# Turning the residual stream into channel order with VectorE's 32 by 32 transposes instead of TensorE's

## The chip, the core and the metric

The kernel runs on one core of one Trainium2 chip. The core's engines work beside each other, each through its own queue in order: TensorE (PE, matmuls; its weight loads are shown as PEld), VectorE (DVE), ScalarE (ACT), GpSimd (POOL) and SyncE (SP, which issues most transfers). They wait for each other through semaphores. The metric is the device time of one execution in microseconds (us), the median over several runs. An engine's memory has 128 partitions; a group of 32 of them is called a quadrant here.

## The reference

Two layers over 256 tokens of width 2048 in float32. Layer 0 mixes tokens with a convolution module, layer 1 with latent attention; after each comes an MLP with a squared ReLU.

```python
for layer in range(DEPTH):                       # DEPTH = 2
    h = rms_norm(x, norm_mixer_g[layer])
    if layer % 2 == 0:
        x = x + conv_module(h, ...)              # ends in u @ w_pw2 + b_pw2
    else:
        x = x + mla(h, ...)                      # ends in o @ w_o
    h = rms_norm(x, norm_mlp_g[layer])
    x = x + jnp.square(jax.nn.relu(h @ w1)) @ w2
return rms_norm(x, final_norm_g)
```

## The kernel before

The residual `x` stays on the chip for the whole run as `xs`, in token order: 128 partitions, two tiles of 128 tokens (t = 0, 1), 2048 channels. A matmul that consumes it needs it in channel order, with channels on the partitions: the buffers `xt`, four of them, one for each block of 512 channels (n = 0 to 3). A block holds four groups k of 128 channels, each with 256 tokens.

Products are computed to float32 accuracy out of parts of lower precision. Each operand x is split into an upper part `hi` = round(x) (ACT, line 161 for weights, line 200 for activations) and a lower part `lo` = x - hi (DVE, line 165 for weights, line 207 for activations that are scaled by a gain). Three matmuls then add up: hi times hi, hi times lo, lo times hi (`mm3`, lines 194 to 196, and lines 409 and 410 in the MLP's first product, where hi and lo lie side by side).

Weights come from memory in units of four groups k of 512 columns (1 MB), by SP into `raw` (three buffers). Each unit is split in two halves, and there are six buffers of halves for `hi` and for `lo` (`WB = 6`). One half is read by 12 matmuls in the products that write tokens on the partitions, and by 16 in the MLP's first product.

Three stages end in a sum onto the residual and turn it into channel order for the next: the convolution module's last product (`conv_w_pw2`), the MLP of layer 0 (the second half of `mlp_w2`) and the attention's output (`mla_w_o`). They share `residual_stage` and `product_A`:

- `product_A` goes over blocks n. For each it computes two accumulators (t = 0, 1) over all k, then DVE adds them to `xs` (`add`, lines 331 and 333).
- `prepare(n)` turns block n into channel order. It is not called at once: the block is put on the list `due`, and `prepare` is called for all blocks on it after the first weight unit of the next block, so that the work stands behind matmuls that don't need it. The last block is turned after the product.
- In the convolution module and in the attention the blocks 0 and 1 are computed before, in one go, and `product_A` is called for blocks 2 and 3 with `due = (0, 1)`: both are turned inside block 2.
- `to_T` (line 252 and following) turns two groups k: four transposes of 128x128 by PE into a bank of PSUM (`tr`), then two upper parts by ACT (line 200) and two lower parts by DVE (line 207), each times the gain of the next norm. A block is two calls: eight transposes, four upper parts, four lower parts.
- `prepare` then also squares the block on ACT (line 345) for the next norm's sum.

In these stages the order of the instructions on each engine's queue is set by a scheduler at build time. The mixers' inner parts are ordered by hand.

At the start of layer 1 some small memsets on DVE (lines 1094 to 1098) and copies on ACT fill the rows for the attention mask; the first product there (`mla_w_in`) takes weights with 576 columns, whose halves hold one group k each.

Of the kernel before, what the change touches and what calls it, by code (L numbers as in the profile page):

```python
# [10 lines left out]
F32 = mybir.dt.float32  # L11
# [7 lines left out]
P = 128  # L19
D = 2048  # L20
KC = D // P
T = 2
S = T * P
FF = 4 * D
NB = 512
# [10 lines left out]
HALVES = 2  # L36
# [41 lines left out]
def trunk_kernel(  # L78
# [26 lines left out]
    nc = tc.nc  # L105
# [27 lines left out]
    def nm(s):  # L133
        uid[0] += 1
        return f"{s}_{uid[0]}"


    def acc_tile():
        return psum["acc"].tile([P, NB], F32, tag="acc", name=nm("acc"))

    def tr_tile():
        return psum["tr"].tile([P, NB], F32, tag="tr", name=nm("tr"))
# [40 lines left out]
    def load_split(srcs, nj):  # L183
        return split(load(srcs, nj), nc.vector)

    def rows(w, k0, nk, c0, n):

        return w[k0 * P : (k0 + nk) * P, c0 : c0 + n].rearrange(
            "(j p) n -> p j n", p=P
        )  # L190
# [7 lines left out]
    def hi_part(ps, hi, scale=1.0):  # L198

        nc.scalar.activation(hi, ps, AF.Copy, scale=scale)  # L200

    def lo_part(ps, hi, lo, scale=None):

        if scale is None:
            nc.vector.tensor_tensor(lo, ps, hi.bitcast(F32), op=ALU.subtract)
        else:
            nc.vector.scalar_tensor_tensor(
                out=lo, in0=ps, scalar=scale, in1=hi.bitcast(F32), op0=ALU.mult, op1=ALU.subtract
            )
# [37 lines left out]
    def to_T(src, k0, hi, lo, gain):  # L247

        pt = tr_tile()
        for j in range(2):  # L250
            for t in range(T):
                nc.tensor.transpose(  # L252
                    pt[:, j * S + t * P : j * S + (t + 1) * P],
                    src[:, t, (k0 + j) * P : (k0 + j + 1) * P],
                    ident,
                )
        ps = [pt[:, j * S : (j + 1) * S] for j in range(2)]
        for j in range(2):
            hi_part(ps[j], hi(k0 + j), gain[:, k0 + j : k0 + j + 1])
        for j in range(2):  # L260
            lo_part(ps[j], hi(k0 + j), lo(k0 + j), gain[:, k0 + j : k0 + j + 1])
# [4 lines left out]
    xs = main.tile([P, T, D], F32, name="xs")  # L266
# [26 lines left out]
    g_mix, g_mlp, b_pw1, b_dw, ln_g, ln_b, g_q, g_kv = cols  # L293
    g_mix = [g_mix[:, 0:KC], g_mix[:, KC:]]
    g_mlp = [g_mlp[:, 0:KC], g_mlp[:, KC:]]


    xt_cx, xt = [ExitStack()], []

    def right_pool(name, bufs):  # L300

        xt_cx[0].close()
        xt_cx[0] = ExitStack()
        return xt_cx[0].enter_context(tc.tile_pool(name=name, bufs=bufs, side="right", reuse_waits="tile"))
# [3 lines left out]
    def open_xt(name):  # L308
        pool = right_pool(name, 1)
        xt[:] = [  # L310
            pool.tile([P, KC // NNB, 2 * S], F32R, name=nm("xt")) for _ in range(NNB)
        ]

    xhl = lambda k: xt[k // 4][:, k % 4, :]
    xh = lambda k: xhl(k)[:, :S]
    xl = lambda k: xhl(k)[:, S:]
# [3 lines left out]
    xh_kt = lambda k, t: xh(k)[:, t * P : (t + 1) * P]  # L320
    xl_kt = lambda k, t: xl(k)[:, t * P : (t + 1) * P]

    def residual_stage(last, gain, r_scale=None):


        ssq = small.tile([P, T, NNB], F32, tag="ssq", name=nm("ssq")) if last else None

        def add(n, ps, t):
            sl = slice(n * NB, (n + 1) * NB)
            if r_scale is None:  # L330
                nc.vector.tensor_tensor(xs[:, t, sl], ps[t], xs[:, t, sl], op=ALU.add)
            else:
                nc.vector.scalar_tensor_tensor(
                    out=xs[:, t, sl], in0=ps[t], scalar=r_scale[:, t : t + 1], in1=xs[:, t, sl],
                    op0=ALU.mult, op1=ALU.add,
                )

        def prepare(n, only=None):
            sl = slice(n * NB, (n + 1) * NB)
            if last:  # L340
                if gain is not None:
                    for j in range(2):
                        to_T(xs, 4 * n + 2 * j, xh, xl, gain)
                for t in range(T) if only is None else [only]:
                    nc.scalar.activation(scratch, xs[:, t, sl], AF.Square, accum_out=ssq[:, t, n : n + 1])

        return ssq, add, prepare
# [41 lines left out]
    def mlp(layer, ssq, next_gain, finish=None, before=None):  # L389

        with ExitStack() as cx:
            mp = cx.enter_context(tc.tile_pool(name=f"mp{layer}", bufs=1, reuse_waits="tile"))
            nkh = FF // P // HALVES
            r2 = small.tile([P, T], F32, tag="r2", name=nm("r2"))
            nssq = None
            for hf in range(HALVES):
                hh, hl = [], []
                for g in range(nkh // 4):
                    ps = [acc_tile() for _ in range(4)]
                    c0 = (hf * nkh + 4 * g) * P  # L400
                    for u in range(KC // 4):
                        wj = load_split([rows(mlp_w1[layer], 4 * u, 4, c0, NB)], 4)
                        for j in range(4):
                            k = 4 * u + j
                            wh, wl = wj(j)
                            for b in range(4):
                                bs = slice(b * P, (b + 1) * P)

                                nc.tensor.matmul(ps[b], wh[:, bs], xhl(k), start=k == 0, stop=False)  # L409
                                nc.tensor.matmul(ps[b][:, :S], wl[:, bs], xh(k), start=False, stop=k == KC - 1)  # L410
                    gh = mp.tile([P, 4, S], F32R, tag="gh", name=nm("gh"), bufs=nkh // 4)
                    gl = mp.tile([P, 4, S], F32R, tag="gl", name=nm("gl"), bufs=nkh // 4)
                    for b2 in range(2):
                        v = mp.tile([P, 2, S], F32, tag="v", name=nm("v"), bufs=2)
                        for b in range(2):
                            o = ps[2 * b2 + b]
                            nc.scalar.activation(v[:, b, :], o[:, S:], AF.Copy)  # L417
                            nc.vector.tensor_tensor(v[:, b, :], o[:, :S], v[:, b, :], op=ALU.add)
                        nc.vector.scalar_tensor_tensor(out=v, in0=v, scalar=0.0, in1=v, op0=ALU.max, op1=ALU.mult)
                        bs = slice(2 * b2, 2 * b2 + 2)  # L420
                        nc.scalar.activation(gh[:, bs, :], v, AF.Copy)
                        nc.vector.tensor_tensor(gl[:, bs, :], v, gh[:, bs, :].bitcast(F32), op=ALU.subtract)
                    hh.append(gh)
                    hl.append(gl)
                if hf == 0:
                    r = rms_rstd(ssq, NNB, D, "n")
                    nc.vector.tensor_tensor(r2, r, r, op=ALU.mult)
                nssq, add, prepare = residual_stage(hf == HALVES - 1, next_gain, r2)
                product_A(
                    mlp_w2[layer],  # L430
                    hf * nkh,
                    nkh,
                    lambda k, t: hh[k // 4][:, k % 4, t * P : (t + 1) * P],
                    lambda k, t: hl[k // 4][:, k % 4, t * P : (t + 1) * P],
                    add,
                    prepare,
                    finish=(lambda t: finish(nssq, t)) if finish is not None and hf == HALVES - 1 else None,
                    before=lambda: before(nssq),
                )
            return nssq  # L440


    with ExitStack() as cx:
# [16 lines left out]
        ca = cv.tile([P, KC, S], F32, tag="tok", name="ca")  # L460
# [208 lines left out]
        with tc.manual_schedule():  # L669
# [36 lines left out]
            for t in range(T):  # L706
# [6 lines left out]
                out=ms0[:, 0:1], in0=xmv[:, 0:1], scalar=xmv[:, 0:1], in1=xmv[:, 1:2], op0=ALU.mult, op1=ALU.add  # L713
# [39 lines left out]
            first, last = ((0, 0), (0, 1)), ((1, 0),)  # L753
# [47 lines left out]
            for c in range(1, KC + 1):  # L801
                n = UC * c
# [88 lines left out]
            for m in range(NP):  # L891
# [4 lines left out]
                for j in range(2):  # L896
                    k = 2 * m + j
# [17 lines left out]
                for q in {NP - 3: (0, 1, 4), NP - 2: (5, 2, 3), NP - 1: (6, 7)}.get(m, ()):  # L915
                    t, i = divmod(q, NNB)
                    sl = slice(i * NB, (i + 1) * NB)
                    nc.vector.tensor_tensor(xs[:, t, sl], xs[:, t, sl], b2[:, sl], op=ALU.add)

        ssq, add, prepare = residual_stage(True, g_mlp[0])  # L920
        for b in range(2):
            for t in range(T):
                add(b, ps2[b], t)
# [3 lines left out]
    with tc.tile_pool(name="rt", bufs=1, reuse_waits="tile") as rt:  # L927
# [52 lines left out]
        nc.scalar.activation(cos, an2, AF.Sin)  # L980

    ssq = mlp(0, ssq, g_mix[1])


    with ExitStack() as cx:
# [321 lines left out]
        with tc.manual_schedule():  # L1307
# [9 lines left out]
            for k in range(KC):  # L1317
                u, j = divmod(k, 2)
# [15 lines left out]
            for k in range(KC):  # L1334
                u, j = divmod(k, 4)
# [30 lines left out]
            cq = at.tile([P, T, QR], F32, tag="cx", name="cq")  # L1366
# [28 lines left out]
            for g in range(NG):  # L1395
                for i in range(HG):
                    h = g * HG + i

                    n = -(-len(work) // (HG - i))
# [29 lines left out]
            prefetch()  # L1429

        open_xt("xt1")
        ssq, add, prepare = residual_stage(True, g_mlp[1])
        for b in range(2):
            for t in range(T):
                add(b, ps_o[b], t)
# [3 lines left out]
    with tc.tile_pool(name="fin", bufs=1, reuse_waits="tile") as fp:  # L1439
# [35 lines left out]
        def before(ssq):  # L1475

            for t in range(T):
# [4 lines left out]
                for n in range(NNB - 1):  # L1482
                    gained(t, n)

        mlp(1, ssq, None, finish, before)


# [24 lines left out]
```

## Time and profile before

| | |
|---|---|
| median of 3 runs | 1991.07 us (1990.93 to 1991.36) |
| profiled execution, its own time | 1991.4 us |
| its span, first to last instruction | 1989.6 us |
| granted TensorE clock, mean | 0.998 |
| instructions | 27809 |

The profile is of one execution. Busy time of an engine is time in which it had an instruction at work; matmuls overlap each other, so a row's "mean ns of one" is longer than the distance between two. In a group of rows the columns are line, engine, operation, output and inputs with shapes, count, then busy time in us and mean ns of one, then the idle time of the engine in front of them and what ended it. In a timeline the columns are start, length (of the merged instructions), engine, line, operation, and in brackets the idle time before and what ended it. The view of waits shows who waited for whom: total us, times, longest.

### The profile page before, as it was taken

What the parts mean: (1) busy time and instruction counts of PE and PEld (TensorE: products, weight loads), DVE (VectorE), ACT (ScalarE), POOL (GpSimd) and SP (SyncE); (2) the same over time, 40 slices, a digit from 0 to 9 for tenths busy, and PEclk for the clock granted to TensorE, in tenths of its full rate; (3) what the DMA queues carried; (4) which work ended last, traced back from release to release, by engine and by line L of the source; (5) the groups of instructions that cost most, each with busy time, mean ns of one, the idle gap of its engine ahead of it and who ended that gap; (6) DMA issues with size and microseconds to landing.
All of it is one profiled execution on the core that took longest, in us unless ns stands there. A gap on an engine that the chain in (4) does not pass through costs nothing.

```text
span 1989.6 us, 27809 instructions
## 1 busy us (share of the span) xinstructions
PE 1969.4 (99%) x11042; PEld 1728.2 (87%) x11042; DVE 1219.7 (61%) x1796; ACT 973.5 (49%) x1377; POOL 228.0 (11%) x189
## 2 busy tenths in 40 slices
PE   8999999999999999999999999999999999999998
PEld 8999888888888888888899998888888888888886
DVE  6999976566444556655556666556654445665553
ACT  5456755454333444544456655545443334454442
POOL 6999300000000000000001310000000000000000
PEclk9999999999999999999999999999999999999999
DMA  7666465565556666665555445666656566665553
GB/s 240 186 181 185 148 205 180 190 190 190 194 195 196 191 189 189 191 198 182 190 167 161 129 141 187 196 189 190 189 195 197 197 192 189 189 190 194 191 190 106
DMA packets 243585, 367.57 MB, mean 185 GB/s; under 512 B 15480, under 2 KB 89984, under 8 KB 243200
## 3 DMA queue, kind: packets, MB, share of 16 engines
q1 hardware_dynamic: 242416, 363.67, 57.7%
q10 hardware_dynamic: 1040, 2.13, 0.3%
q8 instruction: 86, 1.41, 0.3%
q14 instruction: 43, 0.35, 0.0%
HBM read 363.68 MB, written 2.10 MB: 184 GB/s over the span
## 4 chain that ended last, share of the span: by engine, by line
PE 91%; DVE 6%; ACT 1%; POOL 1%; issue 0%; DMA 0%; ACTq 0%; POOLq 0%; DVEq 0%
PE acc L409 23%; PE acc L194 15%; PE acc L196 15%; PE acc L195 15%; PE acc L410 12%; DVE sum L580 5%; PE acc L500 2%; PE acc L908 2%; PE tr L252 1%; POOL lo L165 1%; PE sum L550 0%; ACT hi L161 0%; PE acc L1286 0%; DMA xs<-in_x 0%; PE acc L1150 0%
## 5 line engine op out<-in xcount | busy, mean ns | idle before, releaser
L165 DVE TENSOR_TENSOR lo<-raw,hi 128x1024 fp32r<-128x1024 f32 (+2 forms) x630 | 760.7, 1211 | 691.0 <-ACT hi L161 679.3
L161 ACT ACTIVATE hi<-raw 128x1024 fp32r<-128x1024 f32 (+1 forms) x696 | 722.9, 1046 | 788.0 <-PE acc L195 446.1
L409 PE MATMUL acc<-xt,hi 128*128 128x512 f32 x2048 | 710.6, 390 | 0.0
L410 PE MATMUL acc<-xt,lo 128*128 128x256 f32 x2048 | 577.7, 282 | 0.0
L409 PEld LDWEIGHTS acc<-xt,hi 128*128 128x128 f32 x2048 | 384.4, 188 | 80.5
L194 PE MATMUL acc<-hi,gh 128*128 128x512 f32 x1024 | 398.6, 389 | 0.0
L196 PE MATMUL acc<-lo,gh 128*128 128x512 f32 x1024 | 398.4, 389 | 0.0
L195 PE MATMUL acc<-hi,gl 128*128 128x512 f32 x1024 | 398.4, 389 | 0.0
L410 PEld LDWEIGHTS acc<-xt,lo 128*128 128x128 f32 x2048 | 387.1, 189 | 0.1
L196 PEld LDWEIGHTS acc<-lo,gh 128*128 128x128 f32 x1024 | 192.2, 188 | 40.3
L194 PEld LDWEIGHTS acc<-hi,gh 128*128 128x128 f32 x1024 | 192.2, 188 | 39.7
L195 PEld LDWEIGHTS acc<-hi,gl 128*128 128x128 f32 x1024 | 192.2, 188 | 39.5
L500 PE MATMUL acc<-xt,hi 128*128 128x256 f32 x1024 | 178.9, 281 | 0.0
L580 DVE SCALAR_TENSOR_TENSOR sum<-ub,w_dw,sum 128x256 f32<-128x256 f32 x395 | 160.4, 484 | 3.9 <-ACT sum L556 2.9
L165 POOL TENSOR_TENSOR lo<-raw,hi 128x1024 fp32r<-128x1024 f32 x66 | 157.4, 2406 | 23.5 <-ACT hi L161 19.5
L500 PEld LDWEIGHTS acc<-xt,hi 128*128 128x128 f32 x1024 | 154.4, 188 | 0.1
L500 PE MATMUL acc<-xt,lo 128*128 128x256 f32 x512 | 138.7, 280 | 0.3 <-POOL lo L165 0.3
L500 PEld LDWEIGHTS acc<-xt,lo 128*128 128x128 f32 x512 | 94.3, 188 | 0.5 <-POOL lo L165 0.5
L1081 POOL MEMSET pad_kv<- 128x8 f32 x1 | 0.1, 105 | 761.8 <-PE acc L196 761.8
L417 ACT ACTIVATE v<-acc 128x256 f32<-128x256 f32 x128 | 46.4, 381 | 25.4 <-PE acc L410 25.4
L194 PE MATMUL acc<-hi,oh 128*128 128x512 f32 x128 | 50.7, 396 | 0.0
L196 PE MATMUL acc<-lo,oh 128*128 128x512 f32 x128 | 50.0, 391 | 0.0
(258 smaller groups left out, 1691.1 us busy)
## 6 DMA issues: line engine op xcount, KB each, us to landing
raw<-in_mlp_w SPq DMA_DIRECT2D x256, 1024.0 KB, 5.1
raw<-in_conv_w_pw SPq DMA_DIRECT2D x62, 512.0 KB, 5.0
raw<-in_conv_w_pw SPq DMA_DIRECT2D x16, 1024.0 KB, 4.9
raw<-in_mla_w_o SPq DMA_DIRECT2D x16, 1024.0 KB, 5.3
raw<-in_mla_w_kv_up SPq DMA_DIRECT2D x8, 1024.0 KB, 5.7
raw<-in_mla_w_in SPq DMA_DIRECT2D x8, 576.0 KB, 3.6
raw<-in_mla_w_in SPq DMA_DIRECT2D x4, 1024.0 KB, 5.0
raw<-in_mla_w_q_up SPq DMA_DIRECT2D x16, 256.0 KB, 3.3
```

The source lines that it names most:

```text
L161: nc.scalar.activation(hi, raw[:, js, :], AF.Copy)
L165: eng.tensor_tensor(lo, raw, hi.bitcast(F32), op=ALU.subtract)
L194: nc.tensor.matmul(ps, sh, mh, start=start, stop=False)
L195: nc.tensor.matmul(ps, sl, mh, start=False, stop=False)
L196: nc.tensor.matmul(ps, sh, ml, start=False, stop=stop)
L252: nc.tensor.transpose(pt[:, j * S + t * P : j * S + (t + 1) * P], src[:, t, (k0 + j) * P : (k0 + j + 1) * P], ident,)
L409: nc.tensor.matmul(ps[b], wh[:, bs], xhl(k), start=k == 0, stop=False)
L410: nc.tensor.matmul(ps[b][:, :S], wl[:, bs], xh(k), start=False, stop=k == KC - 1)
L417: nc.scalar.activation(v[:, b, :], o[:, S:], AF.Copy)
L500: nc.tensor.matmul(pss[c][b][:, :S], w[i][:, bs], (xh, xl)[j](k), start=k == i + j == 0, stop=k == KC - 1 and i == 1,)
L580: nc.vector.scalar_tensor_tensor(out=out, in0=ubs[c][:, w : w + S], scalar=tap(c, w), in1=base, op0=ALU.mult, op1=ALU.add)
L908: nc.tensor.matmul(ps2[b][t], x_kt(k, t), w[:, bs], start=k == g == i == 0, stop=k == KC - 1 and i == len(group) - 1,)
```

## The change

`to_T` is no longer used for the residual. In its place `turn_block` issues, for one block of 512 channels, 16 DVE transposes. A DVE transpose turns squares of 32 by 32; one instruction takes 32 partitions (quadrant a: 32 tokens) and, for one b, the 2 x 4 squares of 32 channels that belong to quadrant b, and writes them to the 32 partitions of quadrant b. All four (a) times four (b) together give the full turn. They write float32 to a buffer in the on-chip memory, `raw`, from which ACT and DVE make upper and lower parts as before. One buffer serves all blocks of a stage: in the convolution module it is the front of `ca`, in the attention `cq`, in the MLP of layer 0 a new tile `turned` of 4 KB for each partition. The transposes that `to_T` makes elsewhere (`ckv`, `cq`) stay with PE, as do all others.

```diff
+    def turn_block(n, gain, raw):
+        for a in range(4):
+            src = xs[32 * a : 32 * a + 32, :, n * NB : (n + 1) * NB].rearrange("p t (k b i) -> p b t k i", b=4, i=32)
+            dst = raw.rearrange("p k (t a j) -> p a t k j", t=T, a=4)[:, a]
+            for b in range(4):
+                nc.vector.transpose(out=dst[32 * b : 32 * b + 32], in_=src[:, b])
+        for j in range(NB // P):
+            k = 4 * n + j
+            hi_part(raw[:, j, :], xh(k), gain[:, k : k + 1])
+            lo_part(raw[:, j, :], xh(k), xl(k), gain[:, k : k + 1])
...
-    def residual_stage(last, gain, r_scale=None):
+    def residual_stage(last, gain, r_scale=None, raw=None):
...
                 if gain is not None:
-                    for j in range(2):
-                        to_T(xs, 4 * n + 2 * j, xh, xl, gain)
+                    turn_block(n, gain, raw)
...
+            turned = None if next_gain is None else mp.tile([P, NB // P, S], F32, name=nm("turned"))
...
-                nssq, add, prepare = residual_stage(hf == HALVES - 1, next_gain, r2)
+                nssq, add, prepare = residual_stage(hf == HALVES - 1, next_gain, r2, turned)
...
-        ssq, add, prepare = residual_stage(True, g_mlp[0])
+        ssq, add, prepare = residual_stage(True, g_mlp[0], raw=ca[:, : NB // P, :])
...
-        ssq, add, prepare = residual_stage(True, g_mlp[1])
+        ssq, add, prepare = residual_stage(True, g_mlp[1], raw=cq.rearrange("p t n -> p (t n)").rearrange("p (k s) -> p k s", s=S))
```

As built, the 16 transposes of a block stand next to each other in DVE's queue, the first of them waiting for the sums, the others for nothing. Within one value of a the destination quadrant b changes at every instruction.

## The prediction

> **What bounds the kernel now.** I read the page first: busy times, the chain, then the costliest groups.
>
> ```profile
> PE 1969.4 (99%) x11042; PEld 1728.2 (87%) x11042; DVE 1219.7 (61%) x1796; ACT 973.5 (49%) x1377; POOL 228.0 (11%) x189
> PE 91%; DVE 6%; ACT 1%; POOL 1%; issue 0%; DMA 0%; ACTq 0%; POOLq 0%; DVEq 0%
> L165 DVE TENSOR_TENSOR lo<-raw,hi 128x1024 fp32r<-128x1024 f32 (+2 forms) x630 | 760.7, 1211 | 691.0 <-ACT hi L161 679.3
> raw<-in_conv_w_pw SPq DMA_DIRECT2D x16, 1024.0 KB, 4.9
> ```
>
> TensorE (PE) is busy all the time and 91% of the chain of waits is PE. VectorE (DVE) is busy 61%; its idle time ends on ScalarE's (ACT's) upper halves, so it waits for work. In the view of waits, PE's waits are few, and those of any length stand in the start of the kernel:
>
> ```profile
> PE tr L699 <- DMA xs<-in_x: 6.8, 1, 6.8
> PE acc L723 <- DVE y L223: 2.2, 1, 2.2
> PE tr L1277 <- DVE pr L1271: 1.2, 2, 1.0
> ```
>
> So an instruction taken from PE shortens the kernel by what it occupied, and DVE work costs nothing until PE waits for a `lo` that DVE gives it. Both have to be priced.
>
> **What is removed.** 96 transposes of 128x128, eight for each of 12 blocks of the residual. Their price is read from the second MLP product, whose blocks of 192 matmuls are the same in both halves of layer 0, except that the second half also turns a block. Each row below is the residual add at a block's end, in the timeline of DVE:
>
> ```profile
> 531.22 1.43 DVE L333 SCALAR_TENSOR_TENSOR xs<-acc,r,xs 128x512 f32<-128x512 f32 x2
> 574.74 1.43 DVE L333 SCALAR_TENSOR_TENSOR xs<-acc,r,xs 128x512 f32<-128x512 f32 x2
> ...
> 882.83 1.43 DVE L333 SCALAR_TENSOR_TENSOR xs<-acc,r,xs 128x512 f32<-128x512 f32 x2
> 927.25 1.43 DVE L333 SCALAR_TENSOR_TENSOR xs<-acc,r,xs 128x512 f32<-128x512 f32 x2
> ```
>
> 574.74 - 531.22 = 43.52 us without, 927.25 - 882.83 = 44.42 us with: 0.90 us for eight, so 12 x 0.90 = **10.8 us** off PE. The 16 half-units of a block (a half-unit is two rows of k, 12 matmuls, one upper half on ACT and one lower half on DVE) take 43.52 / 16 = 2.72 us each.
>
> **What is added.** Each block gets 16 DVE transposes of 32 partitions by 256 elements, 192 in all, in DVE's queue at one spot, one after another. The products after them change only their source, SBUF instead of PSUM. The rows nearest to both:
>
> ```profile
> L165 DVE TENSOR_TENSOR lo<-raw,hi 128x1024 fp32r<-128x1024 f32 x606 | 742.4, 1228 | 672.6 <-ACT hi L161 661.0 <-PE tr L252 9.6
> L207 DVE SCALAR_TENSOR_TENSOR xt<-tr,vecs,xt 128x256 fp32r<-128x256 f32 x48 | 20.0, 477 | 2.1 <-PE tr L252 1.8
> L200 ACT ACTIVATE xt<-tr,vecs 128x256 fp32r<-128x256 f32 x48 | 18.9, 471 | 2.8 <-PE tr L252 2.8
> L532 ACT ACTIVATE tp<-ub,w_dw 128x256 f32<-128x256 f32 x45 | 19.5, 495 | 0.0
> L331 DVE TENSOR_TENSOR xs<-acc,xs 128x512 f32<-128x512 f32 x16 | 10.6, 688 | 2.9 <-PE acc L196 1.7 <-PE acc L908 1.2
> L580 DVE SCALAR_TENSOR_TENSOR ca<-ub,w_dw,sum 128x256 f32<-128x256 f32 x14 | 6.6, 475 | 0.0
> ```
>
> The changed sources cost nothing that matters: on DVE 475 ns (L580, SBUF) against 477 (L207), on ACT 495 (L532) against 471. No transpose on DVE stands in the trace. At one element per step, 1228 - 688 = 540 ns for 512 elements is 1.05 ns an element, so 256 elements take 688 - 270 = 418 ns; the slower kind of operation takes 475. Now how close they follow each other. Where the destination stays, operations overlap (`xt`, four in 1.65 us below, so (1.65 - 0.477) / 3 = 0.39 us apart). Here the destination quadrant changes at every step (b is the inner loop), and one place shows what that does, the end of the line below, where layer 1 begins:
>
> ```profile
> 1016.09 1.44 DVE L333 SCALAR_TENSOR_TENSOR xs<-acc,r,xs 128x512 f32<-128x512 f32 x2 [0.79 <-PE acc L196]
> 1017.45 0.75 DVE L165 TENSOR_TENSOR lo<-raw,hi 128x576 fp32r<-128x576 f32 x1
> 1018.71 0.55 DVE L1094 MEMSET scratch<- 64x256 f32 x2 [0.51 <-ACT scratch L345]
> ...
> 1021.07 0.11 DVE L1098 MEMSET scratch<- 1x64 f32 x1
> 1021.23 0.11 DVE L1097 MEMSET scratch<- 1x64 f32 x1
> 1021.30 0.11 DVE L1098 MEMSET scratch<- 1x64 f32 x1
> 1021.45 1.43 DVE L165 TENSOR_TENSOR lo<-raw,hi 128x576 fp32r<-128x576 f32 x2
> ```
>
> The three memsets write rows 64, 96 and 96, and neither the second nor the third waits for a semaphore. The third starts 0.07 us after the second, before its end; the second, in another quadrant than the first, starts at 1021.23, 0.05 us after the first has ended (1021.18). So I price a transpose as a whole operation plus 0.05: between 418 and 475 lies 445, **T = 0.49 us**. Bounds: below, 0.39 (overlap as `xt`) and at the very least 0.27 (the memset of 256 columns, two in 0.55, which reads nothing); above, 0.74, the 128x512 row's 0.69 plus 0.05, if four-byte squares go at half the rate.
>
> [...]
>
> **Where DVE's work is covered, and where not.** PE has six buffers of halves. ACT refills one when PE lets it go, DVE follows, and PE needs it five half-units later.
>
> *Second MLP product of layer 0, three blocks.* Nothing else crowds there. Behind a block's adds (1.4 us) DVE does one `lo` (1.2), then 16T = 7.8, then the seventh half's `lo`: done 11.7 us after the block's end, needed at 6 x 2.72 = 16.3; the eighth follows the products of `xt` (1.65) at 14.4, needed at 19. Cost zero up to T of about 0.78.
>
> *Conv output and attention output, after their first two blocks.* Two blocks are turned inside the one block that follows, eight halves long. The place in conv, from the timelines of PE, DVE and ACT (attention's repeats it):
>
> ```profile
> 263.39 0.39 PE L194 MATMUL acc<-hi,sh 128*128 128x512 f32 x1
> ```
> ```profile
> 262.16 1.22 DVE L165 TENSOR_TENSOR lo<-raw,hi 128x1024 fp32r<-128x1024 f32 x1
> 263.29 1.88 DVE L331 TENSOR_TENSOR xs<-acc,xs 128x512 f32<-128x512 f32 x3
> 265.08 1.22 DVE L165 TENSOR_TENSOR lo<-raw,hi 128x1024 fp32r<-128x1024 f32 x1
> ...
> 271.04 1.65 DVE L207 SCALAR_TENSOR_TENSOR xt<-tr,vecs,xt 128x256 fp32r<-128x256 f32 x4
> ...
> 288.11 1.23 DVE L165 TENSOR_TENSOR lo<-raw,hi 128x1024 fp32r<-128x1024 f32 x1 [0.17 <-ACT hi L161]
> 290.83 1.23 DVE L165 TENSOR_TENSOR lo<-raw,hi 128x1024 fp32r<-128x1024 f32 x1 [1.50 <-ACT hi L161]
> ```
> ```profile
> 278.85 1.06 ACT L161 ACTIVATE hi<-raw 128x1024 fp32r<-128x1024 f32 x1 [1.66 <-PE acc L195]
> ```
>
> PE starts the block at 263.39, the adds end at 265.17. The built program then has on DVE: 16 transposes, the sixth half's `lo` (1.14 to the next start), four products (1.65), the seventh `lo` (1.14), 16 transposes (they reuse the buffer those products have read), the eighth `lo` (1.23). It ends at 265.2 + 5.16 + 32T; PE needs it at 263.39 + 7 x 2.72 = 282.43. PE waits 32T - 12.07 = 3.6 us.
>
> What is late next: after that `lo` DVE has the ninth (1.14), products (1.65), the tenth (1.14), an add (0.60), the eleventh (1.14), an add (0.60), the twelfth (1.14), 16 transposes of the third block, the thirteenth (1.23): 8.64 + 16T, against five halves, 13.6 us. PE waits 16T - 4.96 = 2.9 us. After that DVE needs 1.14 for each 2.72 and catches up; the fourth block is turned behind the sixth half of the MLP, as harmlessly as above. Per place 6.5 us, two places **13.0 us**. ACT's products stand in its queue behind the transposes and ahead of later upper halves, which are due later still; SP's loads wait for a `lo` up to 8 us more, and land in 4.9 us for a use 16 us on. Both stay covered.
>
> *Start of layer 1's attention.* The last block of the MLP is turned when halves are short, one row of k each:
>
> ```profile
> 1016.58 0.29 PE L194 MATMUL acc<-hi,xt 128*128 128x288 f32 x1
> ...
> 1019.96 0.29 PE L194 MATMUL acc<-hi,xt 128*128 128x288 f32 x1
> ...
> 1021.55 0.29 PE L194 MATMUL acc<-hi,xt 128*128 128x288 f32 x1
> ```
>
> A row of k is 12 matmuls, 1021.55 - 1019.96 = 1.59 us, so row 6 is due at 1016.58 + 6 x 1.587 = 1026.10. DVE: transposes from 1018.2, memsets 0.54, products 1.65, small memsets about 0.5, `lo` 0.76: 1021.65 + 16T. PE waits 16T - 4.45 = **3.4 us**; in the old order it waited for none.
>
> **The sum.** 13.0 + 3.4 - 10.8 = +5.6 us; as a function of T, 112T - 49.3, which is zero at T = 0.44. The profiled execution took 1991.4 us, 1.8 of it outside its span of 1989.6, and would become 1997.0. The median of the runs is 0.33 lower: **1996.7 us**, 0.28% slower.
>
> **Rivals.** *Faster: transposes overlap.* [...] Then 0.4 + 1.3 at each of two places and 1.8 at the third: 5.2 - 10.8 = -5.6, 1985.5 us; at T = 0.27 only the 10.8 us remain, 1980.3. It turns at T = 0.44. For it speaks `xt`'s pitch, against it the memset at 1021.23. *No change:* T from 0.404 to 0.476, between -4 and +4 us, at 0.44 1991 us: the plain operation's 0.418 plus 0.05 lies in it. *Four-byte squares at half rate:* T = 0.74: 11.6 + 6.9 at two places, 7.4 at the third: 44.4 - 10.8 = +33.6, 2024.7 us. Nothing in the trace speaks for it; nothing excludes it. *PE gains nothing,* because its transposes fill gaps: then 16.4 us are lost, 2007.5. The 43.52 against 44.42 us speaks against it.
>
> **Chances.** A measurement of this kernel tells 0.2%, 4 us, from no change. Forecast (T 0.476 to 0.65): 0.44; half rate: 0.09; nothing gained on PE: 0.03; together slower 0.56. Between the bounds: 0.20. Faster: 0.24. The forecast's own range is 1995 to 2015; with cases of both signs the range reaches from 1983 (T = 0.36) to 2016, leaving the half rate and the memset's price outside.
>
> **What would show it.** Sixteen transposes starting each 0.05 us after the last has ended, 0.44 us long; PE waits for `lo` at the eighth and thirteenth half after the conv and attention pairs, about 3.6 and 2.9 us, and one of 3.4 at row 6 of attention's first product; none in the MLP's product, whose blocks are 43.52 us apart in both halves. Wrong would be: transposes that overlap, waits of PE elsewhere, or blocks still 44.42 us apart.

## The result, and the profile after

The changed kernel takes 1997.89 us (median of 7 runs, 1996.46 to 1999.24), the kernel before beside it 1991.14 (1990.93 to 1991.36). The ratio is 1.0034, 95% interval 1.0024 to 1.0043: slower by a third of a per cent, 1.2 us above the forecast. The profiled execution took 1997.89 us, its span is 1996.1, 6.5 more than before.

The page's busy times of after:

```profile
PE 1963.4 (98%) x10946; PEld 1721.5 (86%) x10946; DVE 1297.0 (65%) x1988; ACT 973.0 (49%) x1377; POOL 228.0 (11%) x189
```

PE has 96 instructions fewer and 6 us less busy time, in a longer span: it now waits. The view of waits has two rows that were not there before (total us, times, longest):

```profile
PE acc L196 <- DVE lo L165: 9.4, 5, 2.7
...
PE acc L422 <- DVE v L431: 3.6, 2, 3.3
```

The timeline of PE gives their places; the bracket is the idle time before the instruction:

```profile
284.30 0.50 PE L196 MATMUL acc<-lo,sh 128*128 128x512 f32 x1 [1.60 <-DVE lo L165]
299.97 0.50 PE L196 MATMUL acc<-lo,sh 128*128 128x512 f32 x1 [1.76 <-DVE lo L165]
...
340.25 0.76 PE L422 MATMUL acc<-xt,hi 128*128 128x512 f32 x1 [3.27 <-DVE v L431]
...
1031.46 0.40 PE L196 MATMUL acc<-lo,xt 128*128 128x288 f32 x1 [2.68 <-DVE lo L165]
...
1256.88 0.50 PE L196 MATMUL acc<-lo,oh 128*128 128x512 f32 x1 [1.60 <-DVE lo L165]
1272.55 0.50 PE L196 MATMUL acc<-lo,oh 128*128 128x512 f32 x1 [1.74 <-DVE lo L165]
```

Five of the six stand where the prediction put them: two behind the conv pair, two behind the attention pair, one at the start of layer 1's attention. The one at 340.25, in the MLP's first product, was not expected.

The transposes, by the view of their line and in the timeline of DVE, with the adds of two blocks of the MLP:

```profile
L307 DVE STREAM_TRANSPOSE ca<-xs x64: 423/436/442, 264.7 to 321.5; 32x256 f32<-32x256 f32 x64
```
```profile
264.74 7.18 DVE L307 STREAM_TRANSPOSE ca<-xs 32x256 f32<-32x256 f32 x16
...
314.80 7.18 DVE L307 STREAM_TRANSPOSE ca<-xs 32x256 f32<-32x256 f32 x16
...
887.78 1.43 DVE L346 SCALAR_TENSOR_TENSOR xs<-acc,r,xs 128x512 f32<-128x512 f32 x2
...
931.30 1.43 DVE L346 SCALAR_TENSOR_TENSOR xs<-acc,r,xs 128x512 f32<-128x512 f32 x2
```

One takes 436 ns (median of 64); sixteen take 7.18 us, so they start (7.18 - 0.436) / 15 = 0.450 us apart, each 0.014 us after the last has ended. And 931.30 - 887.78 = 43.52 us: the MLP's blocks lost their 0.90 us of transposes and paid nothing for it.

Last, the granted clock. The windows of after (in order: stretch, its length, busy time and count on PE, PEld, DVE, ACT and POOL, then the clock, the DMA share, GB/s):

```profile
300.00:302.00 2.00, 2.00 (x9) 1.63 (x10) 2.00 (x4) 1.35 (x3) 0.00 (x0) 1.00 0.00 0
```
```profile
340.00:341.00 1.00, 0.75 (x2) 0.69 (x3) 1.00 (x4) 0.47 (x2) 0.00 (x0) 0.56 1.03 201
341.00:342.00 1.00, 1.00 (x5) 0.81 (x4) 0.97 (x3) 0.00 (x0) 0.00 (x0) 0.50 0.90 264
342.00:343.00 1.00, 1.00 (x6) 0.90 (x5) 0.42 (x1) 0.00 (x0) 0.00 (x0) 0.50 1.01 377
343.00:344.00 1.00, 1.00 (x6) 0.86 (x6) 0.00 (x0) 0.98 (x2) 0.00 (x0) 0.73 0.60 223
```
```profile
1033.00:1034.00 1.00, 1.00 (x7) 1.00 (x6) 1.00 (x2) 0.97 (x3) 0.00 (x0) 0.51 0.69 106
1034.00:1035.00 1.00, 1.00 (x6) 1.00 (x6) 0.83 (x2) 0.20 (x1) 0.00 (x0) 0.50 0.96 373
1035.00:1036.00 1.00, 1.00 (x6) 1.00 (x6) 0.00 (x0) 0.02 (x1) 0.00 (x0) 0.50 0.94 237
1036.00:1037.00 1.00, 1.00 (x8) 1.00 (x7) 0.31 (x1) 1.00 (x2) 0.00 (x0) 0.78 0.90 291
```

Behind the waits at 340.25 and 1031.46, though not behind the one at 299.97, TensorE runs at half its clock (0.50). The first stretch begins at 341 - 2 x 0.44 = 340.12 and ends at 343 + 2 x 0.27 = 343.54, 3.42 us; the second lasts from 1033.02 to 1036.44. Priced by the clock, each loses half its length, 1.7 us. The starts of the matmuls around the second give a little less: they are 0.24 us apart from 1033.24 to 1036.12 and 0.133 apart before, from 1032.09 to 1032.89, so it loses (0.24 - 0.133) / 0.24 of its length, 1.5 us.

| span after minus before, us | forecast | measured |
|---|---|---|
| transposes off PE | -10.8 | -10.8 (0.90 for each of 12 blocks) |
| conv and attention pairs | +13.0 | +6.7 (1.60 + 1.76 + 1.60 + 1.74) |
| start of layer 1's attention | +3.4 | +2.7 |
| start of the MLP | 0 | +3.3 |
| half clock | 0 | +3.4 (2 x 1.7, by the clock) |
| sum | +5.6 | +5.3 |

The spans differ by 6.5. The remaining 1.2 us lie mostly in the waits themselves. The bracket counts idle time from the end of a matmul, but matmuls overlap, so that a wait costs more from start to start:

```profile
282.08 0.39 PE L194 MATMUL acc<-hi,sh 128*128 128x512 f32 x1
282.31 0.39 PE L195 MATMUL acc<-hi,sl__117 128*128 128x512 f32 x1
```

The next one, with the bracket of 1.60, starts at 284.30 (above): 284.30 - 282.31 = 1.99 us instead of 0.23 (282.31 - 282.08): 1.76 us for an idle time of 1.60. Six waits at 0.16 more are 1.0 us, and the second wait in the row of line 422, at 1306.56, has 0.4.

### The profile page after: what moved, and what is told of

It reads as the page before. It is cut to its first block, busy times and chain, and to the rows that moved or that the text cites. A ratio compares the mean times of both kernels' runs of the same rounds, so it can differ in the third digit from the quotient of the medians.

```text
span 1996.1 us, 27744 instructions
## 1 busy us (share of the span) xinstructions
PE 1963.4 (98%) x10946; PEld 1721.5 (86%) x10946; DVE 1297.0 (65%) x1988; ACT 973.0 (49%) x1377; POOL 228.0 (11%) x189
## 4 chain that ended last, share of the span: by engine, by line
PE 77%; DVE 4%; ACT 1%; DMA 1%; issue 0%; POOL 0%; ACTq 0%; DVEq 0%; SPq 0%
PE acc L422 22%; PE acc L196 14%; PE acc L195 14%; PE acc L194 14%; PE acc L423 12%; DVE cq L307 1%; DVE lo L165 1%; DMA raw<-in_mlp_w 1%; DVE xt L207 0%; ACT hi L161 0%; DVE turned L307 0%; PE acc L1299 0%; PE acc L1163 0%; PE acc L1164 0%; PE acc L1165 0%
## 5 line engine op out<-in xcount | busy, mean ns | idle before, releaser
L165 POOL TENSOR_TENSOR lo<-raw,hi 128x1024 fp32r<-128x1024 f32 x66 | 157.7, 2415 | 23.2 <-ACT hi L161 19.4
```

The source lines that it names most:

```text
L165: eng.tensor_tensor(lo, raw, hi.bitcast(F32), op=ALU.subtract)
```

## The experiments

Each time is the median of several runs, but for three with one run, marked so. The kernel before, beside them, took 1991.06, 1991.03 and 1991.08 us.

### Which blocks cost, and which gain

`mlp_only`: only the MLP of layer 0 uses the new transposes, the mixers keep `to_T`.

```diff
-                    turn_block(n, gain, raw)
+                    if r_scale is not None:
+                        turn_block(n, gain, raw)
+                    else:
+                        for j in range(2):
+                            to_T(xs, 4 * n + 2 * j, xh, xl, gain)
```

> Only the four blocks of layer 0's MLP are turned by VectorE; the eight blocks behind conv and attention go back to TensorE. Theory of separate waits: 4 x 0.90 = 3.6 us off PE, no wait behind conv, at the MLP's start or behind the attention's output; at the start of layer 1's attention the wait of 2.7 us stays, and the half clock behind it (3.4 us long, 1.7 us lost): +0.8 us, 1991.9. Rival, that each turned block costs its share wherever it stands (6.8 us / 12 = 0.57 each): +2.3 us, 1993.4, with waits of PE spread over the MLP's blocks, whose ends are then not 43.52 us apart.

Measured 1991.76 us, ratio 1.0002 (0.9993 to 1.0011). One wait for `lo` is left, in the timeline of PE:

```profile
1026.08 0.51 PE L196 MATMUL acc<-lo,xt 128*128 128x288 f32 x1 [2.69 <-DVE lo L165]
```

Four blocks gain 3.6 us; the wait of 2.69 and the half clock behind it (3.41 us long, from 1026.21) take 4.4. The waits belong each to its own place, and the one at 340.25 belongs to the conv module, not to the MLP's blocks.

`mlp_three`: the same without the MLP's last block (`if r_scale is not None and n < NNB - 1`).

> Blocks 0 to 2 of layer 0's MLP by VectorE, all others by TensorE. Theory of separate waits: 3 x 0.90 = 2.7 us gained and nothing paid, 1988.4, no wait of PE for a lower half anywhere, no half clock between the kernel's start and end. Rival of a cost for each block: +1.7 us, 1992.8.

Measured 1988.98 us, ratio 0.9989 (0.9979 to 0.9998). PE has no wait for `lo` and no half clock in mid-kernel; three blocks off PE's path are worth 2.1 us of the 2.7 expected; the 0.6 us between were not traced. Where a block's turn fits behind matmuls, it gains.

`even`: in the mixers blocks 0 and 2 as well, so that no two turns follow each other (`(n < NNB - 1) if r_scale is not None else n % 2 == 0`).

> Blocks 0 to 2 of the MLP and blocks 0 and 2 behind conv and attention by VectorE, so that no two turns follow each other inside eight halves and none stands at a stage's start. Theory of separate waits: 7 x 0.90 = 6.3 us gained, nothing paid, 1984.8, faster than both kernels. Rival of a cost for each block: 7 x 0.57 = +4.0 us, 1995.1. If only part of the cover is there, waits of PE for a lower half at the eighth or thirteenth half after conv's first two blocks, each below 1.7 us.

Measured 1987.79 us, ratio 0.9985 (0.9976 to 0.9993), 3 us above what was expected. No wait for `lo` is left, but the view of waits has a new row:

```profile
PE tr L252 <- DVE xs L344: 3.0, 2, 1.6
```

These are PE's own transposes of the fourth block, which wait for the add whose sum they turn. The place behind conv in the timelines of PE, DVE and ACT, first of before, then of `even`:

```profile
309.69 0.40 PE L409 MATMUL acc<-xt,hi 128*128 128x512 f32 x1
...
308.04 1.23 DVE L165 TENSOR_TENSOR lo<-raw,hi 128x1024 fp32r<-128x1024 f32 x1 [1.49 <-ACT hi L161]
```
```profile
307.50 0.40 PE L426 MATMUL acc<-xt,hi 128*128 128x512 f32 x1
309.50 0.44 PE L252 MATMUL tr<-ident,xs 128*128 128x128 f32 x2 [1.60 <-DVE xs L344]
...
307.61 1.23 DVE L165 TENSOR_TENSOR lo<-raw,hi 128x1024 fp32r<-128x1024 f32 x1 [1.53 <-ACT hi L161]
308.75 1.28 DVE L344 TENSOR_TENSOR xs<-acc,xs 128x512 f32<-128x512 f32 x2
...
306.52 2.06 ACT L161 ACTIVATE hi<-raw 128x1024 fp32r<-128x1024 f32 x2 [1.88 <-DMA raw<-in_mlp_w]
```

The order in the queues is the same in both kernels: PE's transposes stand behind the first matmul of the next product, and DVE's add behind a lower half. What differs is that lower half. Before, it starts 1.65 us ahead of that matmul (308.04 and 309.69), in `even` 0.11 behind it (307.61 and 307.50), because its upper half on ACT had waited 1.88 us for weights that landed late. The turn of the third block holds up the lower halves, and with them the weights, and the last add comes late. That the late loads come from the turn is argued, no run separates it. The 3 us are this row: 1.6 here and 1.4 at the same place behind the attention.

### Why one transpose waits for the other

`two_halves`: each transpose as two of half the size, neighbours in the same quadrants.

```diff
             for b in range(4):
-                nc.vector.transpose(out=dst[32 * b : 32 * b + 32], in_=src[:, b])
+                for t in range(T):
+                    nc.vector.transpose(out=dst[32 * b : 32 * b + 32, t], in_=src[:, b, t])
```

> Each of the 16 transposes of a block is issued as two of half the size (32 partitions by 128 elements, token tile t innermost), so that two neighbours share the quadrant they read and the quadrant they write; the computation is the same. It asks why a transpose starts only after the one before it has ended (436 ns long, one every 0.45 us). Theory, the quadrant is why: within a pair the second starts before the first has ended, between pairs it waits for the end. A half-size one, at 1.05 ns an element, is about 0.30 us, and a pair takes about 0.45 us as the single one does; the 32 together take 7.2 to 7.6 us. Rival, every transpose waits for the one before it whatever the quadrants: no overlap anywhere, 32 times (0.30 + 0.014) = about 10 us a block, and PE's waits in the conv and attention pairs grow from 1.6 and 1.7 us to 7 and 4.5.

The view of the line, and the timeline of DVE, over stretches that end a little later each time: it shows when the first four transposes end (start of the first, then the time to the end of the last):

```profile
L308 DVE STREAM_TRANSPOSE ca<-xs x128: 256/277/308, 264.7 to 326.4; 32x128 f32<-32x128 f32 x128
```
```profile
264.66 0.29 DVE L308 STREAM_TRANSPOSE ca<-xs 32x128 f32<-32x128 f32 x1
264.66 0.48 DVE L308 STREAM_TRANSPOSE ca<-xs 32x128 f32<-32x128 f32 x2
264.66 0.80 DVE L308 STREAM_TRANSPOSE ca<-xs 32x128 f32<-32x128 f32 x3
264.66 0.99 DVE L308 STREAM_TRANSPOSE ca<-xs 32x128 f32<-32x128 f32 x4
```

The ends are 0.19 us apart within a pair and 0.32 between pairs, and one takes at least 0.256 us: within a pair they overlap, between pairs they don't. So what overlaps is what the theory said, but the size is not: a pair takes 0.51 us instead of 0.45, the 32 take 8.14 instead of 7.2 to 7.6 (10 without overlap). The extra 0.96 us a block was dear: one run took 2016.33 us, with seven waits for `lo` (21.7 us in all, the longest 5.8), and more of them with the half clock behind (mean granted clock 0.993, in after 0.996).

`b_outer`: the loops over a and b exchanged; four transposes in a row write the same quadrant and read four different ones.

```diff
-        for a in range(4):
...
-            for b in range(4):
+        for b in range(4):
+            for a in range(4):
```

> The two loops over quadrants are exchanged: the quadrant that is written now stays for four transposes, and the quadrant that is read changes at every one; the computation is the same. Theory A, a change of the quadrant that is read holds a transpose as well as a change of the one that is written: one every 0.45 us as before, 7.18 us for 16, and PE waits as in the changed kernel (1.6 and 1.7 us in the pairs, 2.7 at the start of layer 1). Theory B, only the written quadrant counts: twelve of sixteen overlap and come every 0.36 to 0.39 us (a pitch of xt's products), 16 take about 6.2 us, and the pairs' first wait shrinks to nothing (32 times 0.39 less 12.07 is 0.4, and what was measured stood 0.7 below that formula).

The timeline of DVE, same place:

```profile
264.92 7.17 DVE L307 STREAM_TRANSPOSE ca<-xs 32x256 f32<-32x256 f32 x16
```

Theory A: the pitch is the same, PE's waits are the same (9.4 us in five), one run took 1999.81 us with more half clock (mean granted clock 0.994). With the quadrant that is read changing at every transpose, 16 take 7.17 us; with the one that is written changing, 7.18. Every one of the 16 pairs of quadrants occurs once, so in any order of the loops one of the two changes at each step.

### The wait at the start of the MLP

What is different there shows in the timelines of ACT, first of before, then of after:

```profile
311.67 0.40 ACTq L930 DMA_DIRECT2D pos_i<-in_positions  x1
...
328.37 0.24 ACT L980 ACTIVATE cos<-an 128x64 f32<-128x64 f32 x1
332.02 1.08 ACT L417 ACTIVATE v<-acc 128x256 f32<-128x256 f32 x3 [0.74 <-PE acc L410]
```
```profile
322.01 0.51 ACT L200 ACTIVATE xt<-ca,vecs 128x256 fp32r<-128x256 f32 x1 [4.74 <-DVE ca L307]
322.10 0.40 ACTq L943 DMA_DIRECT2D pos_i<-in_positions  x1
...
339.12 0.26 ACT L993 ACTIVATE cos<-an 128x64 f32<-128x64 f32 x1 [0.84 <-DVE an L992]
339.28 1.19 ACT L430 ACTIVATE v<-acc 128x256 f32<-128x256 f32 x4
```

ACT's products of the fourth block wait for the transposes. Behind them in ACT's queue stand the small loads for the attention's sine and cosine tables; DVE's arithmetic for the tables follows the loads; and ahead of the copies that free the first accumulators of the MLP (line 430) stands the cosine. The loads and the cosine come 10 to 11 us later than before, the copies 7, and PE waits for an accumulator.

`tables_later`: the tables are held back until the fourth column group of the MLP's first product.

```diff
-    with tc.tile_pool(name="rt", bufs=1, reuse_waits="tile") as rt:
+    def tables(gate):
...
         nc.vector.tensor_copy(pos, pos_i)
+        nc.vector.scalar_tensor_tensor(out=pos, in0=gate, scalar=0.0, in1=pos, op0=ALU.mult, op1=ALU.add)
...
                     hl.append(gl)
+                    if mid is not None and hf == 0 and g == 3:
+                        mid(gl[:, 0, :T].bitcast(F32))
```

> The changed kernel, with the tables of sine and cosine (some 33 small VectorE operations and four ScalarE ones) held back until the MLP's fourth group of columns is done (an added product with zero makes them wait for it; their values stay the same). Theory: the wait of 3.3 us in the MLP's second group comes from the turned fourth block and the tables standing in VectorE's and ScalarE's queues ahead of the accumulators' release; without the tables there it is gone, and with it the half clock behind it (1.7 us): about 5 us less, 1992.9. Rival, that the wait comes from weights which arrive late (the transfers stood still around 320 us): the wait stays, at least 1996.

Measured 1996.72 us, ratio 1.0027 (1.0018 to 1.0036): by its time, the rival. The view of waits:

```profile
PE acc L422 <- DVE v L431: 0.7, 2, 0.4
```

The wait of 3.3 us is gone (0.7 in two are left), but the adds at the ends of two blocks of the second product now start at 532.16 and 576.11: 43.95 us apart instead of 43.52, eight times. One thing had changed that was not meant to: the buffers of the tables live longer, and the MLP's buffers, with them the operands `gh` and `gl` of the second product, stand 1216 bytes further in every partition. Two runs separate this.

`shift_only`: the changed kernel with 1216 bytes of padding ahead of the MLP's buffers.

```diff
+    with tc.tile_pool(name="rt_pad", bufs=1) as rt_pad:
+        rt_pad.tile([P, 304], F32, name="rt_pad")
+        ssq = mlp(0, ssq, g_mix[1])
```

> The changed kernel with 1216 bytes of padding ahead of the MLP's buffers in layer 0, nothing else: no table is held back. Theory, the place of gh and gl sets the pace of the second product: its blocks in layer 0 are 43.95 us apart as in tables_later (43.52 in the changed kernel), and eight blocks cost 3.4 us, about 2001. Rival: 43.52 us apart, about 1998.

One run: 2001.07 us. The adds, in the timeline of DVE:

```profile
536.87 1.44 DVE L346 SCALAR_TENSOR_TENSOR xs<-acc,r,xs 128x512 f32<-128x512 f32 x2
580.82 1.44 DVE L346 SCALAR_TENSOR_TENSOR xs<-acc,r,xs 128x512 f32<-128x512 f32 x2
```

43.95 us: the place alone does it.

`tables_safe`: `tables_later` with the buffers moved on to 4096 bytes.

```diff
+    rt.tile([P, 720], F32, name="rt_pad")
     def tables(gate):
```

> The run tables_later again (sine and cosine tables of the attention held back to the fourth column group of the MLP's first product), with 2880 bytes of padding that move the MLP's buffers of layer 0 from 1216 to 4096 bytes beyond their place in the changed kernel; no other difference. Theory: tables_later kept only 1.2 of the 5 us because its buffers gh and gl stood 1216 bytes further, and the second product's matmuls ran 1% slower for it (43.95 us a block). Now the blocks are 43.52 us apart again, the MLP's early wait and its half clock stay away, and the time is 1992.9. Rival: the slower blocks came from the tables' own work or the changed order, not from the place of the buffers: again 43.95 us a block and 1996 or more.

Measured 1993.72 us (1991.84 to 1994.47), ratio 1.0012 (1.0002 to 1.0021), against 1997.89 for the changed kernel: of the 5 us that the wait and its half clock were priced at, 4.2 come back. The second wait of the conv pair, in the timeline of PE:

```profile
300.04 0.50 PE L196 MATMUL acc<-lo,sh 128*128 128x512 f32 x1 [1.78 <-DVE lo L165]
```

The blocks are 576.33 - 532.81 = 43.52 us apart again, by the same adds. In this profile the half clock follows the wait of 1.78 us (its window stands in the last section), which in the changed kernel's profile it did not.

### Taking the other work off DVE

`pool_lo`: in the two mixers' output products GpSimd computes the second lower half of each weight unit.

```diff
-        parts = [split_half(raw, h, eng) for h in range(2)]
+        parts = [split_half(raw, h, eng2 if h and eng2 is not None else eng) for h in range(2)]
...
-                wjs.append(load_split([rows(w, k_lo + 4 * u, 4, n * NB, NB)], 4))
+                wjs.append(load_split([rows(w, k_lo + 4 * u, 4, n * NB, NB)], 4, nc.gpsimd if nk == KC else None))
```

> In the changed kernel, the lower half of the second half of each weight unit in the conv output and attention output products is computed on GpSimd, which there has nothing else to do (2.4 us each there, one every 5.4 us), and no longer on DVE (1.23 us). Theory: PE's waits in the pairs (1.60 and 1.76 us, 3.3 a place) are nothing but DVE's queue being too long, by the work of less than two lower halves. With at least three taken off before the late one, both waits go in both places: 6.7 us less than the changed kernel, about 1991.2; the waits at the start of the MLP and of layer 1's attention, and the half clock behind them, stay. Rival: GpSimd slows DVE down beside it (lower halves or transposes get longer by 10% and more), or its own 2.4 us come too late, and PE waits for GpSimd in place of DVE: 1994 or more.

Measured 1985.89 us (1984.46 to 1987.36), ratio 0.9974 (0.9963 to 0.9984): 12.0 us below the changed kernel, 5.3 more than expected. The waits of PE, and the lower halves in the groups by form:

```profile
PE acc L196 <- DVE lo L165: 2.7, 1, 2.7
PE acc L422 <- DVE v L431: 1.6, 2, 1.0
```
```profile
L165 DVE TENSOR_TENSOR lo<-raw,hi 128x1024 fp32r<-128x1024 f32 x590 | 721.7, 1228 | 606.6 <-ACT hi L161 604.5
L165 POOL TENSOR_TENSOR lo<-raw,hi 128x1024 fp32r<-128x1024 f32 x82 | 200.7, 2468 | 156.2 <-ACT hi L161 152.4 <-DMA stage<-in_norm_mlp_g 3.8
```

The four waits behind the pairs are gone. DVE's lower halves take the same 1228 ns. GpSimd's mean is 2468, in after 2415; the longest took 6.7 us, in after 2.45, and PE waits for GpSimd as in after, once, 0.3 us (line 513). The surplus is the MLP's start, in the timeline of DVE:

```profile
307.62 7.18 DVE L307 STREAM_TRANSPOSE ca<-xs 32x256 f32<-32x256 f32 x16
```

The fourth block is turned at 307.62 instead of 314.80, because DVE and PE reach it earlier, the tables come earlier, and that wait shrinks from 3.3 to 1.0 us and starts no half clock. The waits behind the pairs, 6.7 us of idle time, and 2.3 of this wait with its half clock (1.7) are 10.7 of the 12.0; 0.16 more for each of the four pair waits, from start to start, adds 0.6. So that wait had the same cause, one stage on.

`pool_att`: also rows 6 to 9 of layer 1's first product.

```diff
-                parts[n, h] = split_half(raws[n], h, nc.vector)
+                parts[n, h] = split_half(raws[n], h, nc.gpsimd if n in (3, 4) else nc.vector)
```

> The run pool_lo, and in the first product of layer 1's attention the lower halves of rows 6 to 9 on GpSimd too (two memsets that stood ahead of them in its queue are moved behind the product); the computation is the same. Theory: the wait of 2.7 us at row 6 and the half clock behind it (1.7 us) come only from row 6's lower half standing behind the sixteen transposes in DVE's queue. On GpSimd it needs no transpose and is done by about 1017, four us ahead of its use: no wait, no half clock, 1985.9 - 4.4 = 1981.5, with all twelve blocks turned by DVE and close to the whole 10.8 us gained. Rival: the wait passes on to the first row that is left with DVE (row 10) or to ScalarE's upper halves, which stand behind the products of the turned block: a wait of 1 us and more stays, and 1984 or more.

Measured 1981.77 us (1981.52 to 1982.06), ratio 0.9953 (0.9940 to 0.9967). The waits of PE, the timeline of POOL at the place, and a window:

```profile
PE acc L422 <- DVE v L431: 1.4, 2, 1.0
```
```profile
1013.62 4.36 POOL L165 TENSOR_TENSOR lo<-raw,hi 128x576 fp32r<-128x576 f32 x3 [719.82 <-ACT hi L161]
```
```profile
1026.00:1031.00 5.00, 5.00 (x40) 5.00 (x39) 3.44 (x5) 2.63 (x5) 0.00 (x0) 1.00 0.53 164
```

GpSimd does the lower halves while DVE turns the block (from 1012.48, 7.17 us). No wait for `lo` is left in the view of waits, the clock stays at 1.00, and all twelve blocks are turned by DVE. This version beats both kernels, by 9.3 us the one before: of the 10.8 us taken off PE, 1.4 go to what is left of the waits at the start of the two MLPs (1.0 and 0.4).

`before_pool`: the same two edits in the kernel before.

> The kernel before, with the same lower halves moved to GpSimd as in pool_att and nothing else: the residual is turned by TensorE. Theory: there no wait of PE came from DVE in these places, so nothing is gained, 1991.0 within 1 us, and what pool_att gains comes from the change itself once its waits are covered. Rival: moving lower halves helps by itself (DVE is short of time in places that the view of waits doesn't show): 1988 or less.

Measured 1991.18 us, ratio 1.0000 (0.9991 to 1.0010). By themselves they gain nothing; the 9.3 us are the change's own.

## Why the prediction was right, point by point

- *10.8 us off PE.* Right. The blocks are 43.52 us apart in both halves of the MLP, and `pool_att` shows the whole gain once the waits are away.
- *T = 0.49 us.* A little high. The operation was 436 ns (445 assumed, the author's estimate between two rows of other operations, 418 and 475), and the gap behind it 0.014 us, not the 0.05 of the memset: 0.45. That is 112 x 0.04 = 4.5 us of the sum, and it lies in the range that the prediction gave to "no change" (0.404 to 0.476), not in the forecast's (0.476 to 0.65). What decided between the forecast and the rival of overlap was right: each transpose starts after the one before it has ended. The order of the loops changes nothing in it (`b_outer`, 16 in 7.17 us), and where both quadrants stay, as within a pair in `two_halves`, two overlap (ends 0.19 us apart, at least 0.256 us for one).
- *MLP's three blocks free.* Right: `mlp_three` gains 2.1 us (2.7 at 0.90 a block) with no wait.
- *Pairs.* Right place, wrong size: 13.0 forecast, 6.7 measured. With T = 0.45 the formulas give 2.3 and 2.2 a place; 1.60 and 1.76 were measured as idle time, 0.16 more each from start to start. The first formula also had the lower half due 0.45 us too early: the first two matmuls of a half (282.08 and 282.31 above) read its upper half alone. The cause, DVE's queue, is shown by `pool_lo`.
- *Start of layer 1's attention.* Right: 16 x 0.45 - 4.45 = 2.75, measured 2.68; `pool_att` removes it by taking the lower halves of rows 6 to 9 out of the queue.
- *The step that failed:* "the fourth block is turned behind the sixth half of the MLP, as harmlessly as above". DVE's lower halves were indeed in time there; what was late were ACT's products, and behind them in ACT's queue the loads and copies that feed tables and accumulators. The prediction said of ACT only that its upper halves were due later. It cost 3.3 us.
- *SP's loads "stay covered".* Not everywhere: ACT waits for weights that landed late, in after 4.93 us ahead of 306.29, where PE has no wait for it, and in `even` 1.88 us ahead of the late add.
- *Not priced:* the half clock behind two of the waits, 3.4 us by the clock.
- *A misread row.* Of the three waits of PE that the prediction puts at the kernel's start, the one of line 1277 stands in the attention (at 1109.93 and 1115.96). Nothing rests on it.

The right total is partly luck. At the measured T the prediction's own formula gives 112 x 0.45 - 49.3 = +1.1 us, which it counted as "no change"; the two terms that it lacked, 6.7 us together, less 2.4 for the pairs' being shorter than the formula, plus the 1.2 that idle time leaves out, bring that to the measured 6.5. So a T that was too high stood in for two terms that were missing. What it did get right is the shape: a gain of 10.8 that is eaten where DVE is crowded, and five of the six places.

## What to carry to other kernels

Before moving work to an engine that is idle on average, price it at the places where it will stand in that engine's queue, and follow what stands behind it in the queues of the engines that wait for it, small loads and table work included. When it doesn't fit, move something else out of that place rather than give the change up: here twenty lower halves on an idle GpSimd turned +0.34% into -0.47%. And price a wait of TensorE with the clock it may lose behind it (1.5 to 1.7 us a time here).

## What the runs showed of the hardware that was not expected

*The half clock follows some waits, and not others of the same length.* In after, half clock begins at 15.86, 340.12, 1033.03 and, until the end, 1992.17: the clocks of the windows 15.80 to 15.90, 340.10 to 340.20, 1033.00 to 1033.10 and 1992.10 to 1992.20 are 0.79, 0.61, 0.65 and 0.87. The first three stretches last 3.41 us each, and the four begins are 324.26, 692.91 and 959.14 us apart, 95, 203 and 281 times 3.413. On that grid the wait of 1.76 us (298.21 to 299.97) is cut by a border at 299.16 into 0.95 and 0.81 us, and costs no clock. In `tables_safe` the window

```profile
301.00:302.00 1.00, 1.00 (x5) 0.82 (x4) 1.00 (x4) 0.42 (x1) 0.00 (x0) 0.66 0.00 0
```

puts the begin at 302 - 2 x 0.34 = 301.32 and the grid's last stretch at 297.91 to 301.32: the whole wait of 1.78 us lies in it, and the half clock follows. In after, the one of 1.60 us (282.70 to 284.30) also lies whole in a stretch, 282.09 to 285.50, and none follows. PE is busy for 1.81 us of that stretch, and for 1.56 of the one ahead of the half clock at 1033.03 (1029.61 to 1033.02). So of these stretches the one with 1.60 us of idle time has no half clock behind it, and those with 1.78 and 1.85 have one; that the idle share decides is the author's reading. It doesn't hold throughout: in `b_outer` two waits of the same length went both ways (timeline of PE, then windows):

```profile
300.15 0.50 PE L196 MATMUL acc<-lo,sh 128*128 128x512 f32 x1 [1.77 <-DVE lo L165]
...
1273.49 0.50 PE L196 MATMUL acc<-lo,oh 128*128 128x512 f32 x1 [1.77 <-DVE lo L165]
```
```profile
301.00:303.00 2.00, 2.00 (x11) 1.65 (x10) 2.00 (x6) 0.53 (x1) 0.00 (x0) 1.00 0.33 80
1274.00:1275.00 1.00, 1.00 (x5) 0.76 (x5) 1.00 (x3) 0.87 (x1) 0.00 (x0) 0.77 0.00 0
```

The second begins a half clock at 1275 - 2 x 0.23 = 1274.54, and the whole wait (1271.72 to 1273.49) lies in the stretch before, from 1271.13. On the same grid the first wait (298.38 to 300.15) lies whole in 298.32 to 301.73, and the clock stays. It begins 0.06 us behind a border; whether that counts is open. So the same wait costs 1.5 to 1.7 us of clock in one place and nothing in another. That fits the spread of the changed kernel's runs (2.8 us, against 0.4 before): the two at 1996.5 and 1996.6 us have a mean granted clock of 0.998, the five longer ones 0.995 or 0.996. Where the half clock stood in them was not traced.

*The pace of matmuls changed with the place of their operands.* With the MLP's buffers, `gh` and `gl` among them, 1216 bytes further, a block of the second product takes 43.95 us instead of 43.52, 1%; with 4096 bytes it stays at 43.52. Which of the addresses matter was not tried.
